# Own slots for the copies of the moved convolution taps, and the layer norm's mean spread one projection later

## The chip, the core and the metric

The kernel runs on one core of one Trainium2 chip. The core has five engines, each with a queue of its own that is worked off in order: PE (TensorE, matrix products), DVE (VectorE), ACT (ScalarE), POOL (GpSimd) and SP (SyncE, which here only issues DMAs). POOL issues the DMAs that add to their destination. They all work on one on-chip memory; 16 DMA engines move data. The metric is the device time of one execution in microseconds (us), lower is better.

## The reference

Two layers. Layer 0 mixes positions by two groups of convolutions, layer 1 by stick-breaking attention; each is followed by a gated ConvFFN. Sequence 1024, width 1024, everything in float32. The change lies in the mixer of layer 0:

```python
def conv_mixer(h, w_in, a_dw_w, a_dw_b, a_ln_g, a_ln_b, b_dw_w, w_out):
    p = h @ w_in
    a_val, a_gate, b_gb, b_gc, b_h = jnp.split(
        p, [D_A, 2 * D_A, 2 * D_A + D_B, 2 * D_A + 2 * D_B], axis=-1)
    a = causal_dwconv(a_val * jax.nn.sigmoid(a_gate), a_dw_w, a_dw_b)   # width 31
    a = jax.nn.silu(layernorm(a, a_ln_g, a_ln_b))
    b = b_gb * causal_dwconv(b_gc * b_h, b_dw_w)                        # width 3
    return jnp.concatenate([a, b], axis=-1) @ w_out
```

D_A and D_B are 512, so the input projection has 2560 columns, 20 blocks of 128.

## The kernel before

Channels lie on the 128 partitions, the 1024 positions along the free axis. A tensor of 128 x 1024 floats is one slot; `Mem` hands out 38 slots by number (t16 to t53; the names in the rows carry slot and allocation, t44_551 is slot 44), oldest freed first. Who writes into a slot waits until the previous owner's last reader is done, a DMA included.

Every float32 product is made of three passes (`mm3`, lines 644 to 646) over a high and a low part of each operand. So each weight slot is split: ACT casts the high part (line 628), DVE subtracts to get the low part (line 629). `W.pump` keeps loads and splits some projections ahead.

`mixer0` runs the 20 projections n = 0 to 19, here p0 to p19; one is 48 matmuls into one of three PSUM tiles (b0, b1, bb0, taken in turn, so that pn needs the tile of p(n-3) read out). p0 to p7 are gate and value of the four channel blocks j of group A: after each value, `conv_taps` queues the 31-wide convolution of the block. 20 of its taps are multiply-adds on DVE (`dtap`, line 838). 10 are moved off it: two initialise two sums, eight (`mtap`, lines 841 to 845) are a scaled copy by ACT into a slot (line 843) and a DMA issued by POOL that adds the slot to one of the two sums in turn (line 844); a merge adds one sum to the other (line 848), and `fin` (line 858) adds them to DVE's part. I call the four convolutions c0 to c3 and the eight added copies of one its adds 1 to 8. An add waits for the add before it on the same sum, so two are in flight.

p8 to p19 are the three projections of each block of group B: gc is copied by ACT (line 1102), h is multiplied in by DVE (line 1104) and convolved (lines 815, 819), gb is multiplied in (line 1109), then the result is split. Before p17, `b_out` puts the first three blocks of B through their part of the output projection.

The layer norm of A goes in four steps after projections: `ln0` after p14 finishes all taps and sums the four blocks (lines 1009 to 1011), `ln1` after p15 spreads the mean over the partitions by a matmul with ones (line 1016, `spread`), subtracts it (line 1032), squares and sums; `ln2` after p16 spreads the variance; `ln3` after p17 spreads the inverse root (line 1016), scales (1052), applies swish (1054, 1055, 1057) and splits the four parts of A. After p19 `back_all` multiplies these four parts and the last part of B by their output weights, eight row tiles one after the other.

The engines' instructions stand in an order that a scheduler wrote at build time; each engine keeps to it. Line numbers below line 843 are one to three higher in the changed kernel.

Of the kernel before, what the change touches and what calls it, by code (L numbers as in the profile page):

```python
# [152 lines left out]
class Up:  # L153
# [12 lines left out]
    def __init__(self, k, l):  # L166
        self.k, self.l = k, l
        self.raw, self.S, self.A, self.a1, self.done1 = {}, {}, {}, {}, {}
        self.rb, self.ys, self.T = [None] * 4, {}, {}
# [40 lines left out]
    def split2(self, f):  # L210
# [8 lines left out]
        m.free(v)  # L219
        self.A[f] = s12, s34, a22  # L220

# [145 lines left out]
    def block(self, f):  # L367

        k, m, nc = self.k, self.k.m, self.k.nc
        if f + 2 < NF and f + 2 not in self.raw:  # L370
            self.load(f + 2)
        if f not in self.A:
            self.split2(f)
# [4 lines left out]
        lo, hi = slice(0, 512), slice(512, 1024)  # L378
        (s12h, s12l), (s34h, s34l), a22 = self.A.pop(f)
        H, L, H3, L3, A2 = [m.ap(s) for s in (s12h, s12l, s34h, s34l, a22)]  # L380
# [238 lines left out]
class Kern:  # L619
# [203 lines left out]
    def conv_taps(self, j, u, acc, sums):  # L823


        nc, m = self.nc, self.m
        w = [self.const(self.col["aw"] + k * NJ + j) for k in range(CW)]
        U, A, B = m.ap(u), m.ap(acc), [m.ap(s) for s in sums]
        shifts = list(range(1, CW))
        moved, dve = shifts[:MOVED_TAPS], shifts[MOVED_TAPS:]  # L830

        nc.scalar.activation(A, U, AF.Identity, scale=w[CW - 1], bias=self.const(self.col["ab"] + j))
        for s, b in zip(moved, B):
            nc.gpsimd.memset(b[:, 0:s], 0.0)
            nc.scalar.activation(b[:, s:], U[:, :S - s], AF.Copy, scale=w[CW - 1 - s])

        def dtap(s):
            nc.vector.scalar_tensor_tensor(out=A[:, s:], in0=U[:, :S - s], scalar=w[CW - 1 - s],
                                           in1=A[:, s:], op0=ALU.mult, op1=ALU.add)

        def mtap(s, b):
            t = m.alloc()
            nc.scalar.activation(m.ap(t)[:, :S - s], U[:, :S - s], AF.Copy, scale=w[CW - 1 - s])
            nc.gpsimd.dma_start(out=b[:, s:], in_=m.ap(t)[:, :S - s], accum_op=ALU.add)
            m.free(t)

        def merge():
            nc.gpsimd.dma_start(out=B[0], in_=B[1], accum_op=ALU.add)
            m.free(sums[1])

        for s in dve:
            self.dq.append(lambda s=s: dtap(s))
        for i, s in enumerate(moved[2:]):
            self.pq.append(lambda s=s, b=B[i % 2]: mtap(s, b))
        self.pq.append(merge)

        def fin():
            nc.vector.tensor_tensor(out=A, in0=A, in1=B[0], op=ALU.add)
            m.free(u)
            m.free(sums[0])  # L860
            self.conv_done += 1

        self.fq.append((len(self.dq) + self.dn, len(self.pq) + self.pn, fin))
# [118 lines left out]
    def mixer0(self):  # L982
        nc, m, a = self.nc, self.m, self.a
# [18 lines left out]
        self.open_psum("ps0b", 1, 2)  # L1002

        accs, bparts, aparts = [], [], []
        W.reserve = 4


        def total(xs):
            nc.gpsimd.tensor_tensor(out=m.ap(s1), in0=xs[0], in1=xs[1], op=ALU.add)
            nc.vector.tensor_tensor(out=m.ap(s2), in0=xs[2], in1=xs[3], op=ALU.add)  # L1010
            nc.vector.tensor_tensor(out=m.ap(s1), in0=m.ap(s1), in1=m.ap(s2), op=ALU.add)
# [8 lines left out]
        def ln0():  # L1020
            nonlocal s1, s2, A
            self.pop_bg(200, 200)
            assert self.conv_done == NJ
            A = [m.ap(s) for s in accs]
            s1, s2 = m.alloc(), m.alloc()
            total(A)
# [34 lines left out]
            m.free(s2)  # L1061

        s1 = s2 = A = None
        ln = [ln0, ln1, ln2, ln3]
        def b_out(wi):
            W.pump(wi[-1])
            ws = [W.views(q) for q in wi]
            acts = [(m.ap(h), m.ap(l)) for h, l in bparts]
            self.back_all(acts, ws, lambda t: self.pop_bg(2, 1))
            for q in wi:  # L1070
                W.done(q)
            while bparts:
                for q in bparts.pop():
                    m.free(q)

        for n in range(20):
            if n == pb:
                b_out([pb + q for q in range(nb)])
            i = n if n < pb else n + nb
            W.pump(i)  # L1080
            if i < 2:
                ps = self.first[i]
            else:
                ps = self.big()
                for c in range(2):
                    self.proj_chunk(ps, W.views(i), c)
            W.done(i)
            if n < 8:
                j = n // 2
                if n % 2 == 0:  # L1090
                    sg = m.alloc()
                    nc.scalar.activation(m.ap(sg), ps, AF.Sigmoid)
                else:
                    nc.vector.tensor_tensor(out=m.ap(sg), in0=ps, in1=m.ap(sg), op=ALU.mult)
                    acc, sums = m.alloc(), [m.alloc() for _ in range(2)]
                    accs.append(acc)
                    self.conv_taps(j, sg, acc, sums)
            else:
                j, q = divmod(n - 8, 3)
                if q == 0:  # L1100
                    gc = m.alloc()
                    nc.scalar.copy(out=m.ap(gc), in_=ps)
                elif q == 1:
                    nc.vector.tensor_tensor(out=m.ap(gc), in0=ps, in1=m.ap(gc), op=ALU.mult)  # L1104
                    cv = m.alloc()
                    self.conv3(m.ap(cv), m.ap(gc), [self.const(self.col["bw"] + k * NJ + j) for k in range(3)], None)
                    m.free(gc)
                else:
                    nc.vector.tensor_tensor(out=m.ap(cv), in0=ps, in1=m.ap(cv), op=ALU.mult)
                    bparts.append(self.split(cv))  # L1110
            self.pop_bg(6, 3)
            if 14 <= n < 18:
                ln[n - 14]()

        gain = self.load_gain(a["ffn_norm_g"][0:1, :].rearrange("o d -> (o d)"))
        W.reserve = 2
# [506 lines left out]
```

## Time and profile before

| | |
|---|---|
| median of 3 runs | 2321.15 us (2319.4 to 2325.52) |
| the profiled execution, device time | 2319.02 us |
| its span in the trace | 2317.2 us |
| mean granted TensorE clock | 0.993 |
| busy share of the span | PE 96%, DVE 75%, ACT 54%, POOL 24% |

The profile's times count from the span's start. The device time holds 1.8 us around the span. A row of a timeline gives start and duration, engine, line, operation, output and inputs, and in brackets how long the engine had been idle and what released it.

### The profile page before, as it was taken

Reading aid. Unit: us, or ns where it says so; the run is one execution under the profiler, and the core shown is the slowest. Engines: PE = TensorE matmul, PEld = TensorE weight load, DVE = VectorE, ACT = ScalarE, POOL = GpSimd, SP = SyncE. Lnnn points to the kernel's source line nnn. Section 1 sums busy time; section 2 is a strip of 40 time slices with the busy share of each in tenths; the row PEclk is TensorE's granted clock in tenths of the full one; section 3 lists DMA queues with packets and bytes.
Section 4 is the critical chain, followed back from the end, with each engine's and each line's share of the span. In section 5 each row is a group of like instructions: output and inputs, shape, how many; then the busy total and the mean of one; then the engine's idle time right before and its main releaser. Section 6 shows DMA issues by size and latency. Waiting matters only on the chain. (4 is left out here: it accounts for less than half of the span.)

```text
span 2317.2 us, 29706 instructions
## 1 busy us (share of the span) xinstructions
PE 2232.6 (96%) x11076; PEld 1908.4 (82%) x11076; DVE 1726.5 (75%) x2023; ACT 1262.6 (54%) x1978; POOL 561.8 (24%) x551
## 2 busy tenths in 40 slices
PE   8998999999999999999999999989999999999999
PEld 8886887888788888889999999978777888888887
DVE  6879457877686887556888888887668777778863
ACT  6433246555555543436677677765566565655341
POOL 2221012111111000035555555562121121110000
PEclk9999999999999999999999999999999999999999
DMA  5984146767676494321111110034476767666812
GB/s 178 190 174 99 35 127 144 191 144 193 148 186 155 146 386 168 103 80 28 37 28 37 37 37 10 28 106 152 130 162 166 192 149 196 145 177 249 332 51 109
DMA packets 247826, 313.00 MB, mean 135 GB/s; under 512 B 12557, under 2 KB 170753, under 8 KB 247681
## 3 DMA queue, kind: packets, MB, share of 16 engines
q1 hardware_dynamic: 214977, 238.32, 31.0%
q0 software_dynamic: 32704, 72.78, 17.7%
q8 instruction: 87, 1.43, 0.2%
q14 instruction: 58, 0.48, 0.1%
HBM read 181.14 MB, written 60.82 MB: 104 GB/s over the span
## 5 line engine op out<-in xcount | busy, mean ns | idle before, releaser
L199 POOL DMA_DIRECT2D t<-t x176 | 155.8, 978 | 701.2 <-ACT t L194 271.3
L628 ACT CAST t<-t 128x1024 fp32r<-128x1024 f32 x178 | 184.9, 1048 | 223.9 <-DMA hs<-t 62.0
L819 DVE SCALAR_TENSOR_TENSOR t<-t,cst,t 128x1023 f32<-128x1023 f32 (+1 forms) x184 | 236.1, 1286 | 81.9 <-ACT t L817 76.7
L629 DVE TENSOR_TENSOR t<-t,t 128x1024 fp32r<-128x1024 f32 x178 | 219.1, 1237 | 101.0 <-ACT t L628 47.2
L1274 DVE TENSOR_TENSOR_SCAN t<-t 128x127 f32<-128x127 f32 (+7 forms) x128 | 204.1, 1600 | 6.9 <-ACT t L1265 6.8
L644 PE MATMUL ps1s<-wH,hH 128*128 128x384 f32 x448 | 165.8, 370 | 0.0
L646 PE MATMUL ps0b<-hH,t 128*128 128x512 f32 x396 | 154.6, 391 | 3.5 <-DVE t L629 3.4
L644 PE MATMUL ps0b<-hH,t 128*128 128x512 f32 x396 | 155.8, 395 | 1.9 <-DVE t L1104 1.4
L645 PE MATMUL ps0b<-hL,t 128*128 128x512 f32 x396 | 154.7, 391 | 0.0
L710 POOL TENSOR_TENSOR stat<-stat,mhalf 128x8 f32<-128x8 f32 (+1 forms) x65 | 80.2, 1234 | 299.9 <-DVE stat L709 299.7
L646 PE MATMUL ps1s<-wH,hL 128*128 128x384 f32 x448 | 151.1, 337 | 0.0
L1279 POOL TENSOR_TENSOR t<-t,t 128x639 f32<-128x639 f32 (+1 forms) x64 | 108.6, 1697 | 175.1 <-DVE t L1274 103.7
L645 PE MATMUL ps1s<-wL,hH 128*128 128x384 f32 x448 | 150.9, 337 | 0.0
L817 ACT ACTIVATE t<-t,cst 128x1024 f32<-128x1024 f32 x88 | 109.1, 1240 | 66.3 <-DVE t L392 47.4
L645 PE MATMUL ps2b<-t,t 128*128 128x512 f32 x342 | 133.9, 392 | 3.9 <-DMA t<-t 3.9
L644 PE MATMUL ps2b<-t,t 128*128 128x512 f32 x342 | 134.0, 392 | 3.3 <-ACT t L394 1.6
L646 PE MATMUL ps2b<-t,t 128*128 128x512 f32 x342 | 132.7, 390 | 0.0
L1265 ACT ACTIVATE t<-ps1s 128x512 f32<-128x512 f32 (+1 forms) x192 | 95.4, 497 | 54.7 <-PE ps1s L1261 28.3
L1297 ACT CAST t<-ps1s 128x512 fp32r<-128x512 f32 (+1 forms) x160 | 87.3, 546 | 60.9 <-PE ps1s L1293 53.5
L1298 DVE TENSOR_TENSOR t<-ps1s,t 128x512 fp32r<-128x512 f32 (+1 forms) x160 | 100.2, 627 | 21.0 <-ACT t L1297 18.8
L517 ACT CAST hH<-t 128x1024 fp32r<-128x1024 f32 x64 | 64.4, 1051 | 86.4 <-PE ps0bs L645 19.6
L517 ACT CAST hL<-t 128x1024 fp32r<-128x1024 f32 x64 | 64.3, 1051 | 86.3 <-PE ps2s L645 25.3
(348 smaller groups left out, 6480.7 us busy)
## 6 DMA issues: line engine op xcount, KB each, us to landing
t<-in_ffn_w_up_dram SPq DMA_DIRECT2D x88, 512.0 KB
t<-t POOLq DMA_DIRECT2D x176, 256.0 KB, 4.4
t<-hs SPq DMA_DIRECT2D x66, 512.0 KB
hs<-t SPq DMA_DIRECT2D x60, 512.0 KB
t<-in_ffn_w_down_dram SPq DMA_DIRECT2D x66, 256.0 KB
xd<-t SPq DMA_DIRECT2D x24, 512.0 KB
wr<-in_attn_w_qkv_dram SPq DMA_DIRECT2D x24, 512.0 KB
t<-in_ffn_w_up_dram SPq DMA_DIRECT2D x44, 256.0 KB
```

The source lines that it names most:

```text
L199: nc.gpsimd.dma_start(out=out, in_=src, accum_op=ALU.add)
L517: nc.scalar.copy(out=r(m.ap(h)), in_=src)
L628: nc.scalar.copy(out=r(m.ap(h)), in_=m.ap(src))
L629: (eng or nc.vector).tensor_tensor(out=r(m.ap(l)), in0=m.ap(src), in1=m.ap(h), op=ALU.subtract)
L644: mm(out=ps, lhsT=sH, rhs=mH, start=start, stop=False, skip_group_check=onto)
L645: mm(out=ps, lhsT=sH, rhs=mL, start=False, stop=False, skip_group_check=onto)
L646: mm(out=ps, lhsT=sL, rhs=mH, start=False, stop=stop, skip_group_check=onto)
L817: nc.scalar.activation(dst, src, AF.Identity, scale=wcols[2], bias=bias)
L819: nc.vector.scalar_tensor_tensor(out=dst[:, s:], in0=src[:, :S - s], scalar=wcols[2 - s], in1=dst[:, s:], op0=ALU.mult, op1=ALU.add)
L1274: self.nc.vector.tensor_tensor_scan(out=rev, data0=rev, data1=rev, initial=1.0, op0=ALU.mult, op1=ALU.bypass)
L1279: self.nc.gpsimd.tensor_tensor(out=B[:, 0:n - 1], in0=B[:, 0:n - 1], in1=K[:, 1:n], op=ALU.mult)
L1298: nc.vector.tensor_tensor(out=r(aL), in0=ps[:, 0:pos], in1=aH, op=ALU.subtract)
```

## The change

The scaled copies of `mtap` no longer take and free a slot each: four slots are taken once, before the projections, and used in turn, and are freed when `ln0` begins. Three of the four steps of the layer norm move by one projection: the mean is spread after p16, the variance after p17, the inverse root after p18.

```diff
         def mtap(s, b):
-            t = m.alloc()
+            t = self.copies[self.ncopy % len(self.copies)]
+            self.ncopy += 1
             nc.scalar.activation(m.ap(t)[:, :S - s], U[:, :S - s], AF.Copy, scale=w[CW - 1 - s])
             nc.gpsimd.dma_start(out=b[:, s:], in_=m.ap(t)[:, :S - s], accum_op=ALU.add)
-            m.free(t)
...
         accs, bparts, aparts = [], [], []
+        self.copies, self.ncopy = [m.alloc() for _ in range(4)], 0
         W.reserve = 4
...
             assert self.conv_done == NJ
+            for s in self.copies:
+                m.free(s)
...
-        ln = [ln0, ln1, ln2, ln3]
+        ln = {14: ln0, 16: ln1, 17: ln2, 18: ln3}
...
-            if 14 <= n < 18:
-                ln[n - 14]()
+            if n in ln:
+                ln[n]()
```

The scheduler writes the whole mixer in another order. Three places:

PE, the spreading of the mean. Before, it stands between p15 (tile b1) and p16 (tile b0):

```order
L645 MATMUL ps0b1_72<-hL_67,t30_1393 128x512
L646 MATMUL ps0b1_72<-hH_66,t37_1394 128x512
L1016 MATMUL ps0bb0_548<-t51_1515,tmp_87 128x512 x2
L644 MATMUL ps0b0_71<-hH_66,t47_1458 128x512
L645 MATMUL ps0b0_71<-hL_67,t47_1458 128x512
```

Now it stands behind p16 (tile bb0) and is followed by the first products of `b_out`:

```order
L645 MATMUL ps0bb0_548<-hL_67,t37_1430 128x512
L646 MATMUL ps0bb0_548<-hH_66,t31_1431 128x512
L1017 MATMUL ps0b0_71<-t35_1487,tmp_87 128x512 x2
L644 MATMUL ps0b1_72<-t36_1494,t52_1208 128x512
L645 MATMUL ps0b1_72<-t50_1495,t52_1208 128x512
```

The 48 matmuls of p16 have moved ahead of it.

ACT, the copies of c3 (inputs t26_936 before, t25_926 now) and the splits of weights around them. Before, the high part of p12 (t51_1175) stands eight rows ahead of these, among c2's copies, and here come the copy of p8's result (L1102), c3's copies out of their order, each into a slot of its own, c2's last copy (t36_1169) and the split for p13 (t50_1250):

```order
L1102 COPY t32_1084<-ps0b0_71 128x1024
L843 ACTIVATE t45_1384<-t26_936,cst_177 128x1015
L843 ACTIVATE t44_1387<-t26_936,cst_177 128x1014
L843 ACTIVATE t38_1316<-t26_936,cst_177 128x1016
L843 ACTIVATE t36_1169<-t53_786,cst_177 128x1014
L628 CAST t50_1250<-t37_1101 128x1024
L843 ACTIVATE t36_1310<-t26_936,cst_177 128x1018
```

Now c3's adds 5 to 8 are copied into slots 44 to 47, each of which its adds 1 to 4 read, and the high parts for p12 (t31_1155), p13 and p14 stand behind all of them:

```order
L1105 COPY t35_1069<-ps0b0_71 128x1024
L844 ACTIVATE t44_551<-t25_926,cst_177 128x1017
L844 ACTIVATE t45_552<-t25_926,cst_177 128x1016
L844 ACTIVATE t46_553<-t25_926,cst_177 128x1015
L844 ACTIVATE t47_554<-t25_926,cst_177 128x1014
L628 CAST t31_1155<-t42_1015 128x1024
L628 CAST t36_1227<-t24_1083 128x1024
L628 CAST t42_1295<-t37_1153 128x1024
```

The split for p12 has moved from the copies of c2 to behind the last copy of c3.

DVE, the low part for p12 and the multiplication that reads p9's tile b1. Before, the low part (t33_1176) comes nine rows ahead of it (L1104):

```order
L629 TENSOR_TENSOR t33_1176<-t38_1030,t51_1175 128x1024
L838 SCALAR_TENSOR_TENSOR t24_711<-t36_639,cst_177,t24_711 128x996
L838 SCALAR_TENSOR_TENSOR t42_1006<-t26_936,cst_177,t42_1006 128x1011
L838 SCALAR_TENSOR_TENSOR t41_859<-t53_786,cst_177,t41_859 128x1003
L838 SCALAR_TENSOR_TENSOR t24_711<-t36_639,cst_177,t24_711 128x995
L838 SCALAR_TENSOR_TENSOR t42_1006<-t26_936,cst_177,t42_1006 128x1010
L838 SCALAR_TENSOR_TENSOR t41_859<-t53_786,cst_177,t41_859 128x1002
L838 SCALAR_TENSOR_TENSOR t24_711<-t36_639,cst_177,t24_711 128x994
L858 TENSOR_TENSOR t24_711<-t24_711,t27_712 128x1024
L838 SCALAR_TENSOR_TENSOR t42_1006<-t26_936,cst_177,t42_1006 128x1009
L1104 TENSOR_TENSOR t32_1084<-ps0b1_72,t32_1084 128x1024
```

Now it (t51_1156) comes three rows ahead of it (L1107):

```order
L858 TENSOR_TENSOR t43_709<-t43_709,t31_710 128x1024
L838 SCALAR_TENSOR_TENSOR t32_994<-t25_926,cst_177,t32_994 128x1010
L838 SCALAR_TENSOR_TENSOR t48_852<-t28_782,cst_177,t48_852 128x1001
L629 TENSOR_TENSOR t51_1156<-t42_1015,t31_1155 128x1024
L838 SCALAR_TENSOR_TENSOR t32_994<-t25_926,cst_177,t32_994 128x1009
L838 SCALAR_TENSOR_TENSOR t48_852<-t28_782,cst_177,t48_852 128x1000
L1107 TENSOR_TENSOR t35_1069<-ps0b1_72,t35_1069 128x1024
```

The multiplication and every tap after it now stand behind a split that waits for ACT's cast of t31_1155.

## Rows read from the trace of the kernel before

**Rows 1.** The page's first part: busy time, share of the span and instructions of an engine.
```profile
PE 2232.6 (96%) x11076; PEld 1908.4 (82%) x11076; DVE 1726.5 (75%) x2023; ACT 1262.6 (54%) x1978; POOL 561.8 (24%) x551
```
**Rows 2.** Stretches of the mixer: start:end, length, busy us (instructions) of PE, PE's weight loads, DVE, ACT and POOL, then granted clock, DMA share, GB/s.
```profile
130.00:140.00 10.00, 10.00 (x46) 8.29 (x45) 10.00 (x9) 7.70 (x8) 3.52 (x4) 1.00 1.02 189
...
180.00:190.00 10.00, 6.93 (x30) 5.37 (x30) 10.00 (x7) 0.00 (x0) 3.29 (x2) 1.00 0.73 144
190.00:200.00 10.00, 8.23 (x35) 6.22 (x34) 10.00 (x9) 3.15 (x3) 0.00 (x0) 1.00 0.18 52
200.00:210.00 10.00, 7.45 (x33) 5.82 (x31) 9.87 (x10) 3.95 (x4) 0.00 (x0) 1.00 0.29 87
210.00:220.00 10.00, 6.42 (x12) 3.78 (x13) 9.39 (x9) 2.42 (x3) 0.00 (x0) 0.66 0.07 20
220.00:230.00 10.00, 10.00 (x45) 8.25 (x44) 10.00 (x8) 5.07 (x5) 2.41 (x1) 1.00 0.41 116
```
**Rows 3.** Timeline of PE: the first matmul of p11, of p12 and of p13, the waits after it, the mean's spreading, p16, the first matmul of `b_out`, and the spreading in `ln3` with the matmul after it.
```profile
145.56 0.39 PE L644 MATMUL ps0b<-hH,t 128*128 128x512 f32 x1
156.44 0.39 PE L644 MATMUL ps0b<-hH,t 128*128 128x512 f32 x1
168.22 0.47 PE L644 MATMUL ps0bb<-hH,t 128*128 128x512 f32 x1 [0.74 <-DVE t L1109]
183.50 0.50 PE L646 MATMUL ps0b<-hH,t 128*128 128x512 f32 x1 [3.07 <-DVE t L629]
195.67 0.47 PE L644 MATMUL ps0b<-hH,t 128*128 128x512 f32 x1 [1.43 <-DVE t L1104]
213.58 3.78 PE L1016 MATMUL ps0bb<-t,tmp 128*128 128x512 f32 x4 [6.13 <-DVE t L1011]
216.37 1.42 PE L644 MATMUL ps0b<-hH,t 128*128 128x512 f32 x1
229.14 0.39 PE L644 MATMUL ps0bb<-t,t 128*128 128x512 f32 x1
274.43 1.88 PE L1016 MATMUL ps0bb<-t,tmp 128*128 128x512 f32 x4
275.74 0.79 PE L644 MATMUL ps0b<-hH,t 128*128 128x512 f32 x1
```
**Rows 4.** Who waited for whom from 45 to 240 us: engine, tile, line, what was waited for: us in total, times, longest.
```profile
DVE t L629 <- DMA t<-t: 14.4, 3, 6.6
...
ACT t L843 <- DMA t<-t: 35.4, 11, 8.0
```
**Rows 5.** Timeline of DVE: ten taps in a row, and the sum of the four blocks, for which the mean's spreading waits.
```profile
100.63 11.99 DVE L838 SCALAR_TENSOR_TENSOR t<-t,cst,t 128x1006 f32<-128x1006 f32 x10
...
212.30 1.23 DVE L1011 TENSOR_TENSOR t<-t,t 128x1024 f32<-128x1024 f32 x1
```
**Rows 6.** Timeline of POOL: c0's adds 1 and 2, its merge; c1's add 1 and 5, its merge; c2's adds 1 and 2, its adds 3 and 4.
```profile
53.83 1.96 POOL L844 DMA_DIRECT2D t<-t  x2 [9.59 <-ACT t L843]
80.00 0.88 POOL L848 DMA_DIRECT2D t<-t  x1 [4.47 <-DMA t<-t]
85.10 0.87 POOL L844 DMA_DIRECT2D t<-t  x1 [4.11 <-ACT t L843]
99.55 0.87 POOL L844 DMA_DIRECT2D t<-t  x1 [3.05 <-DMA t<-t]
114.57 0.87 POOL L848 DMA_DIRECT2D t<-t  x1 [5.14 <-DMA t<-t]
115.12 2.16 POOL L844 DMA_DIRECT2D t<-t  x2
122.47 0.87 POOL L844 DMA_DIRECT2D t<-t  x1 [5.18 <-ACT t L1092]
125.04 0.87 POOL L844 DMA_DIRECT2D t<-t  x1 [1.70 <-DMA t<-t]
```
**Rows 7.** The adds' line: time from issue to landing.
```profile
DMA to landing us min/median/max: 4.5/5.7/11.9
```
**Rows 8.** Groups of instructions from 45 to 213 us: count, busy us and mean ns of one, idle time before them.
```profile
L629 DVE TENSOR_TENSOR t<-t,t 128x1024 fp32r<-128x1024 f32 x14 | 17.0, 1220 | 23.6 <-DMA t<-t 14.4 <-ACT t L628 9.2
L1104 DVE TENSOR_TENSOR t<-ps0b,t 128x1024 f32<-128x1024 f32 x2 | 2.4, 1214 | 0.0
L843 ACT ACTIVATE t<-t,cst 128x1021 f32<-128x1021 f32 (+7 forms) x32 | 34.9, 1138 | 35.4 <-DMA t<-t 35.4
L628 ACT CAST t<-t 128x1024 fp32r<-128x1024 f32 x16 | 16.4, 1044 | 42.7 <-DVE t L858 16.2 <-DMA t<-in_conv_w_in_dram 9.3 <-DVE t L1109 8.0
```
**Rows 9.** Timelines of DVE, ACT and PE after the spreading in `ln3` (274.43): scaling, sigmoid, the split of the first part, the low parts of the last part and of a weight, the first matmul of `back_all`.
```profile
276.35 4.61 DVE L1052 TENSOR_TENSOR t<-t,ps0bb 128x1024 f32<-128x1024 f32 x4 [10.51 <-PE ps0bb L1016]
277.60 2.38 ACT L1054 ACTIVATE t<-t,cst 128x1024 f32<-128x1024 f32 x2 [1.96 <-DVE t L1052]
285.56 1.99 ACT L628 CAST t<-t 128x1024 fp32r<-128x1024 f32 x2
296.16 2.35 DVE L629 TENSOR_TENSOR t<-t,t 128x1024 fp32r<-128x1024 f32 x2
297.95 0.39 PE L644 MATMUL ps0bb<-t,t 128*128 128x512 f32 x1
```

## The prediction, made before the changed kernel ran

> **What bounds the kernel now.** I read the profile's first part first: PE is busy 96% of the span and DVE, the next, 75% [rows 1]. A change gains only where PE idles or runs slowly, and loses where it makes PE wait. So I looked for PE's waits where the change works. From the start of b_out at 229.14 until some time after back_all's start at 297.95 there is none; ahead of it there are four [rows 3]: p13 waits 0.74 for L1109, p14 3.07 for a low weight part of DVE, p15 1.43 for L1104, and the mean's spreading 6.13 for L1011 on DVE.
>
> The last costs twice. After it the granted clock is 0.66 in 210:220 [rows 2], a mixture of 1.2 and 2.4 GHz. The spreading takes 2.79 until p16 starts (213.58 to 216.37) against 1.31 for the one in ln3 (274.43 to 275.74), and p16 takes 12.77 (216.37 to 229.14) against 10.88 for p11 (145.56 to 156.44) [rows 3]: 1.48 + 1.89 = 3.4 us of slow clock. The 3.07 wait was followed by a stretch at 1.00 [rows 2].
>
> What could be had at most: p12 to p16 and one spreading at full rate take 5 x 10.88 + 1.31 = 55.7; from p12's start at 156.44 that ends at 212.15, and b_out starts at 229.14. **The headroom is 17.0 us.** Some 11.4 of it are the four waits, 3.4 the clock, the rest slow first matmuls behind waits.
>
> DVE is the engine that is late: it is busy 9.4 to 10 of every 10 us shown from 180 on [rows 2]. Yet between 45 and 240 its low splits waited 14.4 us, three times, for a DMA, at most 6.6 at once, and ACT's copies at L843 waited 35.4 us for DMAs, 11 times [rows 4]. Those are waits for slots that something else had used.
>
> **Own slots: what they remove.** No instruction is added or removed. Each adding DMA now holds a slot that only other copies want, so the splits no longer wait for an add's landing, and the 14.4 us of DVE should go. With DVE that much earlier, the waits of p13 to p15 and of the mean lose their cause.
>
> **The mean one projection later: what it removes.** Now PE may do p16 before the mean. The sum L1011 (213.5 at its end [rows 5]) then has 10.88 us more, so the 6.13 wait and its 3.4 of clock are gone so long as DVE doesn't get much later. These two parts could give the whole 17.0.
>
> **What they add.** The order shows a new chain. ACT's copies for c3's adds 5 to 8 reuse the slots of its adds 1 to 4, and each must wait until its slot's add has landed. The high part for p12 stands behind all four on ACT; the low part stands on DVE just ahead of two taps and L1107, which reads out p9's tile b1, and p12 needs that tile. All later taps are queued behind it too. Before, that split stood among c2's copies. So I need the landing of c3's add 4.
>
> c0's merge is issued at 80.00, and nothing ahead of it moves. A convolution takes 26.2 from its first add to its merge (53.83 to 80.00) or 29.5 (85.10 to 114.57), and the next may start 0.55 later (114.57 to 115.12) [rows 6]. Two more convolutions put c2's merge at 80.00 + 2 x 26.75 = 133.5 at the earliest and 80.00 + 2 x 30.05 = 140.1 at the latest. c3's add 4 is issued 0.55 + 9.92 (115.12 to 125.04 [rows 6]) later, at 144.0 to 150.6, and lands 4.5 to 5.7 after that (minimum and median; maximum 11.9 [rows 7]): 148.5 to 156.3, or 162.5 at worst. I take 156.3, the late end, because the DMA engines had no share left over in 130:140 (1.02 [rows 2]) when c2's adds ran there, and the order puts c3's adds among weight loads.
>
> Behind the landing: a copy 1.14, the high split 1.04, the low split 1.2 [rows 8], two taps at 1.2 [rows 5], L1107 1.2 [rows 8], together 7.0. L1107 ends at 163.3, while PE wants p12 at 156.44: **a wait of 6.9 us**, with bounds of 0 (landing at 148.5: 155.5) and 13.1 (landing at 162.5). p13 needs L1112 of p10, eleven DVE instructions behind L1107: 11 x 1.18 = 13.0, so 176.3 instead of 167.32. That is 9.0 late. The clock probably falls again as after the 6.13 wait, but the slow p12 (163.3 + 12.8 = 176.1) fits into p13's wait. With all 3.4 of clock it would be 163.3 + 10.88 + 3.4 = 177.6, 10.3 late. **I take 9.5 lost**, and nothing lost after p13: L1011 stands 39 instructions behind L1107, 39 x 1.2 = 47, so the sum is ready at 210, and PE arrives at the spreading at 156.44 + 54.4 + 9.5 = 220.3. The 10 us between are also what covers the cost of moving the mean; if DVE were more than 10 us later still, the old wait would return. b_out starts 17.0 - 9.5 = 7.5 earlier than now.
>
> A rule of the Trainium skill, "DMA: Bandwidth & Descriptors", section "Issuing engines are not separate DMA queues", speaks against a quicker chain of adds: DMAs from whichever engine end up on the same 16 DMA engines and interleave, so four slots more buy no more transfer rate. The row that agrees is the share of 1.02 in 130:140 [rows 2]. By that rule the landing is at the late end, as taken; without it, at 148.5, the wait would be nothing.
>
> **The inverse root one projection later: what it costs.** Before, p18 and p19 covered ln3's work between its spreading and back_all. Now only p19 does, which ends 1.31 + 10.88 = 12.2 after the spreading's start. Counted from that start in the trace of before: L1052 at 1.92, the sigmoid at 3.17, the first part's split from 11.13 [rows 9] until 12.2 [rows 8]. In the new order, DVE then takes L1112 of p19, which needs p19's end: 12.2 + 1.2 = 13.4. Seven low splits follow at 1.17 (two in 2.35 [rows 9]): the seventh, the low part of the fourth output weight, ends at 21.6. Ahead of the matmuls that need it PE has 30 of earlier parts, 30 x 0.227 = 6.8 (10.88 over 48), until 12.2 + 6.8 = 19.0. **Cost 2.6.** Bounds: 0 if DVE finds time for splits earlier; 10.7 if it takes as long as before, 22.9 from the spreading to that weight's low part (274.43 to 297.3, the second of the two splits [rows 9]), with nothing between p19's end and it. I take 2.6 because the order does leave those matmuls there.
>
> **Sum.** -17.0 + 9.5 + 2.6 = -4.9. The profiled execution took 2319.0, so 2314.1; the median of the runs is 2.1 above that execution, so **2316**. What a measurement of this kernel can tell from no change is about 0.3%, 7 us.
>
> **The rivals.**
> *No new wait.* The adds run at the quick pace (26.2, landing 4.5), c3's add 4 lands by 149.5, and L1107 is done before PE wants it. Then -17.0 + 2.6 = -14.4: median 2306.7. For it: nothing but adds uses those slots now, and ACT's 35.4 us of waiting [rows 4] were partly what held the adds up, such as the 4.11 ahead of c1's first [rows 6]. Against: the full DMA engines.
> *The tail costs its upper bound*, and own slots only move the wait: -17.0 + 9.5 + 10.7 = +3.2, median 2324.3. For it: ACT and DVE in ln3 depend on each other from step to step. Against: a DVE that is earlier elsewhere.
> *Slower.* c3's adds 2 and 4, in series on one sum, each land only after the maximum, 11.9, instead of 5.7. Then add 4 lands at 156.3 + 2 x 6.2 = 168.7, L1107 ends at 175.7, p13 starts at 188.7, 21.4 late, and the net is -17.0 + 21.4 + 2.6 = +7.0: median 2328.2. The gain is gone from a landing of 161.7 on. For it: landings of 11.9 do occur [rows 7] where loads share the engines. Against: the median is half that, and two in a row are needed.
> That the change doesn't do what it says would need the mean's sum over 10 us later than worked out above; I count that in with the slower one.
>
> "TensorE: Matmul & The Clock Gate" of the Trainium skill, Part 1, has the clock fall to 1.2 GHz when PE has been idle. The trace agrees after the 6.13 wait (0.66 in the next row [rows 2]), while after the 3.07 wait the row stays at 1.00. By that rule the slow clock follows the new 6.9 wait too, which is the 10.3 bound above instead of 9.5: a total of 2317 rather than 2316.
>
> **How the numbers follow.** Forecast 0.50, no new wait 0.25, tail at its bound 0.15, slower 0.10. The forecast lies 2 us short of 0.3% faster, so about 0.13 of its 0.50 falls beyond: faster 0.25 + 0.13 = 0.38. The slower case lies at +7.0, on the bound: with its worse half and a share of the tail's, slower 0.10. Same: the remaining 0.52. The range goes from the quick case's time, 2306, to between the tail's and the slower case's, 2326. The forecast's own is 2312 to 2321 (bounds of the wait and the clock).
>
> **What would show it.** Right: ACT's L844 waiting for an adding DMA between 140 and 157; DVE's L629 waiting many us for ACT's L628 there; PE waiting about 7 us for L1107 at p12's start and again for L1112 at p13's; no wait at the mean's spreading, which starts near 220; b_out near 221.6; a short wait for L629 in back_all's first products. Wrong: p12 starting at 156.4 (the first rival), a wait of some 10 us at back_all (the second), p12 starting beyond 169 or a wait left at the mean (the third).

## The result, and the profile after

The changed kernel is slower: 2331.49 us in the median (2328.38 to 2336.45), against 2322.29 of the kernel before in the same comparison. The ratio is 1.0043, 95% interval 1.0027 to 1.0058. The forecast was 2316 with a range to 2326, so it was wrong in size and in sign. The profiled execution has a span of 2328.5 us, 11.3 more than the one before. I follow the difference by the start of the same matmul in both traces: +2.2 at p11, +17.7 at p12, +3.0 at b_out, +8.5 in the last row tile of back_all. The rest of the 11.3, 2.8 us, gathers far behind the mixer, where nothing was changed; the medians differ by 9.2.

PE of the changed kernel: its waits, the spreading of the mean (230.86) and of the inverse root (289.13). They answer to [rows 3]. Columns: start, duration, engine, line, operation, tiles; in brackets the wait before it and what ended it.

```profile
147.72 0.50 PE L644 MATMUL ps0b<-hH,t 128*128 128x512 f32 x1 [0.42 <-ACT t L1105]
174.14 0.77 PE L644 MATMUL ps0b<-hH,t 128*128 128x512 f32 x1 [15.23 <-DVE t L1107]
187.34 0.39 PE L644 MATMUL ps0bb<-hH,t 128*128 128x512 f32 x1
230.86 1.88 PE L1017 MATMUL ps0b<-t,tmp 128*128 128x512 f32 x4
289.13 1.88 PE L1017 MATMUL ps0b<-t,tmp 128*128 128x512 f32 x4
304.10 0.50 PE L644 MATMUL ps0b<-t,t 128*128 128x512 f32 x1 [1.18 <-DVE t L1112]
306.40 0.50 PE L646 MATMUL ps0bb<-t,t 128*128 128x512 f32 x1 [1.57 <-DVE t L629]
310.94 0.50 PE L645 MATMUL ps0bb<-t,t 128*128 128x512 f32 x1 [0.84 <-DVE t L629]
```

The four waits of before, 11.4 us in all, are gone, the 6.13 at the mean among them. One of 15.2 at p12's start has come in their place, and it costs the clock too: p12 takes 13.20 (174.14 to 187.34) instead of 10.88, and the granted clock, the third number from the right, says why: 0.59 and 0.56 from 160 to 180 (columns as in [rows 2]):

```profile
140.00:150.00 10.00, 9.58 (x43) 7.61 (x42) 7.28 (x7) 3.20 (x3) 2.90 (x4) 1.00 0.59 110
150.00:160.00 10.00, 8.90 (x40) 7.04 (x38) 0.00 (x0) 2.29 (x2) 1.76 (x2) 1.00 1.09 217
160.00:170.00 10.00, 0.00 (x0) 0.00 (x0) 0.72 (x1) 3.96 (x4) 1.75 (x2) 0.59 1.03 228
170.00:180.00 10.00, 5.86 (x16) 4.71 (x17) 10.00 (x10) 2.39 (x3) 2.65 (x3) 0.56 0.75 138
180.00:190.00 10.00, 10.00 (x46) 8.26 (x45) 10.00 (x9) 3.02 (x3) 0.00 (x0) 1.00 0.27 52
```

DVE does nothing at all from 150 to 160, ACT a quarter of the time: neither is short of time, both wait. ACT's timeline (c3's copies 5 to 8, then the high parts for p12 and p13) and DVE's (the low part for p12, two taps, L1107) show the chain, link by link:

```profile
153.67 1.15 ACT L844 ACTIVATE t<-t,cst 128x1017 f32<-128x1017 f32 x1 [6.00 <-DMA t<-t]
157.61 1.14 ACT L844 ACTIVATE t<-t,cst 128x1016 f32<-128x1016 f32 x1 [2.79 <-DMA t<-t]
163.35 1.14 ACT L844 ACTIVATE t<-t,cst 128x1015 f32<-128x1015 f32 x1 [4.60 <-DMA t<-t]
167.18 1.14 ACT L844 ACTIVATE t<-t,cst 128x1014 f32<-128x1014 f32 x1 [2.68 <-DMA t<-t]
168.22 1.97 ACT L628 CAST t<-t 128x1024 fp32r<-128x1024 f32 x2
...
169.28 1.23 DVE L629 TENSOR_TENSOR t<-t,t 128x1024 fp32r<-128x1024 f32 x1 [22.00 <-ACT t L628]
170.42 2.44 DVE L838 SCALAR_TENSOR_TENSOR t<-t,cst,t 128x1009 f32<-128x1009 f32 x2
172.78 1.22 DVE L1107 TENSOR_TENSOR t<-ps0b,t 128x1024 f32<-128x1024 f32 x1
```

Four copies each wait for an add to land, the last until 167.18; the split for p12 follows at 168.22, DVE has waited 22.0 us for it, L1107 ends at 174.0 and p12 starts at 174.14. This is the chain of the prediction; the landing that it waits for comes 10.9 us later than predicted. Where the time went, the adds on POOL say: the first two of a convolution (x2), the third, the merge (L848).

```profile
55.43 1.95 POOL L845 DMA_DIRECT2D t<-t  x2 [3.45 <-ACT t L844]
60.71 0.86 POOL L845 DMA_DIRECT2D t<-t  x1 [3.33 <-DMA t<-t]
74.89 0.89 POOL L845 DMA_DIRECT2D t<-t  x1 [2.08 <-DMA t<-t]
82.35 0.88 POOL L848 DMA_DIRECT2D t<-t  x1 [6.58 <-DMA t<-t]
82.90 2.13 POOL L845 DMA_DIRECT2D t<-t  x2
92.59 0.89 POOL L845 DMA_DIRECT2D t<-t  x1 [7.56 <-DMA t<-t]
...
113.71 0.87 POOL L848 DMA_DIRECT2D t<-t  x1 [4.60 <-DMA t<-t]
114.26 2.15 POOL L845 DMA_DIRECT2D t<-t  x2
121.73 0.87 POOL L845 DMA_DIRECT2D t<-t  x1 [5.31 <-DMA t<-t]
...
146.21 0.89 POOL L848 DMA_DIRECT2D t<-t  x1 [6.00 <-DMA t<-t]
146.75 2.15 POOL L845 DMA_DIRECT2D t<-t  x2
154.23 0.87 POOL L845 DMA_DIRECT2D t<-t  x1 [5.33 <-DMA t<-t]
158.17 0.89 POOL L845 DMA_DIRECT2D t<-t  x1 [3.07 <-DMA t<-t]
```

c0 takes 26.9 from its first add to its merge, c1 30.8, c2 32.0. Within c0, adds follow each other every 2.84 us (60.71 to 74.89, five steps). Where a merge is in flight ahead of a convolution, its third add comes 7.5 to 9.7 after its first; in c0, with no merge ahead, 5.3.

### The profile page after: what moved, and what is told of

Same layout as the page of the kernel before. It is cut to its first block, busy times and chain, and to the rows that moved or that the text cites. A ratio compares the mean times of both kernels' runs of the same rounds, so it can differ in the third digit from the quotient of the medians.

```text
span 2328.5 us, 29722 instructions
## 1 busy us (share of the span) xinstructions
PE 2234.7 (96%) x11076; PEld 1909.1 (82%) x11076; DVE 1726.6 (74%) x2023; ACT 1263.4 (54%) x1978; POOL 563.8 (24%) x551
## 5 line engine op out<-in xcount | busy, mean ns | idle before, releaser
L644 PE MATMUL ps1s<-wH,hH 128*128 128x384 f32 x448 | 165.7, 370 | 0.0
L644 PE MATMUL ps0b<-hH,t 128*128 128x512 f32 x364 | 143.4, 395 | 16.6 <-DVE t L1107 15.2
L646 PE MATMUL ps0b<-hH,t 128*128 128x512 f32 x364 | 142.4, 392 | 0.4 <-DVE t L629 0.3
L645 PE MATMUL ps0b<-hL,t 128*128 128x512 f32 x364 | 142.5, 392 | 0.0
L1300 ACT CAST t<-ps1s 128x512 fp32r<-128x512 f32 (+1 forms) x160 | 87.3, 545 | 61.8 <-PE ps1s L1296 54.4
```

The costliest lines, as they stand in the source:

```text
L644: mm(out=ps, lhsT=sH, rhs=mH, start=start, stop=False, skip_group_check=onto)
L645: mm(out=ps, lhsT=sH, rhs=mL, start=False, stop=False, skip_group_check=onto)
L646: mm(out=ps, lhsT=sL, rhs=mH, start=False, stop=stop, skip_group_check=onto)
```

## The experiments

My theory after the result: the loss is the new chain through ACT's queue (p12's split behind copies that wait for c3's adds), and in addition the late inverse root at back_all. The rivals: the shift of the layer norm alone makes the loss; DVE's time is what counts; the adds are slow because of what else the DMA engines carry.

**The two halves of the change.** The changed kernel with the old places of the layer norm, and the kernel before with the new places:

```
-        ln = {14: ln0, 16: ln1, 17: ln2, 18: ln3}      (e1, slots alone)
+        ln = {14: ln0, 15: ln1, 16: ln2, 17: ln3}

-        ln = [ln0, ln1, ln2, ln3]                      (e2, shift alone, from before)
+        ln = {14: ln0, 16: ln1, 17: ln2, 18: ln3}
...
```

> Own slots, the layer norm where it was before. ACT's order around c3's copies is the one of the changed kernel. If the loss comes from p12's split standing behind c3's copies 5 to 8 (theory): PE waits 13 to 17 us for L1107 at p12's start, as the 15.2 of the changed kernel; later waits (5.2 at p13 to p15, most of the 6.13 at the mean and its 3.4 of clock) are given back; b_out starts 3 to 6 us later than before, back_all has no new wait: 2322 to 2328, 1.001 to 1.002 of before. If the loss comes from the later steps of the layer norm (rival): faster than before by 5 to 10 us, and no wait over 8 us at p12.

> A slot taken for each copy as before, the layer norm's three steps one projection later. Theory: no long wait at p12; the 6.13 wait and its slow clock at the mean vanish (the mean is ready near 213.5, PE reaches it near 218), so b_out starts 9 to 10 us earlier than before; back_all's first products wait as in the changed kernel, where they cost 5.5: a net gain of 4 us (7 with the 2.6 that was predicted for the tail), 0.997 to 0.998 of before. Rival (the shift makes the loss): slower than before by 5 us or more.

e1: 2331.82 us, ratio 1.0033 (1.0020 to 1.0046); at p12 a wait of 14.68 for L1107. e2: 2322.17 us, 1.0000 (0.9991 to 1.0010). So the own slots make the loss, and the rival falls. But e1 is 3.8 above the top of its range. In its trace b_out starts 4.4 later than before, as expected, and the last row tile of back_all is 4.4 later too; the span is 14.9 longer. The other 10 or so gather behind the mixer; why there, no run shows. The mixer's loss is thus only about half of e1's 8.8 in the medians. Nor did the shift gain what I expected of it. PE in e2:

```profile
220.07 1.88 PE L1016 MATMUL ps0b<-t,tmp 128*128 128x512 f32 x4
229.68 0.50 PE L644 MATMUL ps0b<-t,t 128*128 128x512 f32 x1 [1.34 <-DVE t L1032]
...
295.78 0.51 PE L644 MATMUL ps0b<-t,t 128*128 128x512 f32 x1 [1.19 <-DVE t L1109]
298.08 0.50 PE L646 MATMUL ps0bb<-t,t 128*128 128x512 f32 x1 [1.56 <-DVE t L629]
```

The mean waits no more, and b_out starts 7.8 us earlier than before. Then b_out's matmuls wait for tiles that DVE reads late, because it now subtracts the mean beside them, and 5.0 are left at p18 (leaving out one spreading, which comes before p18 there and behind it here). back_all's waits cost 5.4, and nothing is left: its last row tile comes 0.5 later than before.

**Where the tail's cost sits.** The variance is spread straight after b_out, the inverse root after p17 as before; the mean stays after p16. Once without own slots (e5), once in the changed kernel (e10):

```
-        ln = {14: ln0, 16: ln1, 17: ln2, 18: ln3}      (e10; in e5 from [ln0, ln1, ln2, ln3])
+        ln = {14: ln0, 16: ln1, 17: ln3}
...
                 b_out([pb + q for q in range(nb)])
+                ln2()
```

> No own slots; the mean is spread after p16, but the variance straight after b_out (ahead of p17) and the inverse root after p17 as before. If the tail's cost comes from the inverse root standing after p18: no waits at back_all, and the 5 us that shift_only still had in hand at p18 stay: 2316 to 2319, 0.9975 to 0.9985 of before. If the later mean itself is the cost there: no better than shift_only, 0.999 to 1.001.

> The changed kernel, but the variance is spread straight after b_out and the inverse root after p17 as before; own slots and the later mean stay. If the tail's 5.5 us belong to the inverse root standing after p18, and are independent of the wait at p12: the wait of 15 us at p12 stays, no wait at back_all, 2324 to 2327, 1.0005 to 1.002 of before. If back_all's waits come from DVE's lateness after p12: within 2 us of the changed kernel.

e5: 2317.43 us, 0.9980 (0.9966 to 0.9994): faster than before, with no wait at back_all, and 6 us earlier there than before. e10: 2328.52 us, 1.0023 (1.0011 to 1.0035), a median 1.5 above the expected range; it still waits 15.19 at p12, and no longer at back_all. So the tail's cost belongs to the two late steps, the variance after p17 and the inverse root after p18, and not to the later mean or to DVE's lateness after p12. The two were moved together.

**Only the place of p12's split.**

```
-        W.reserve = 4                                  (e3)
+        W.reserve, W.split_ahead = 4, 3
```

> The changed kernel with weights split three projections ahead instead of two; in the order this puts the high part for p12 on ACT ahead of c3's copies, while p9's convolution (L815) stays behind them. Theory: no wait at p12 for L1107; DVE's 22 us wait for ACT's L628 near 147 is gone; p13, whose tile L1112 reads only after that convolution, then waits 5 to 7 us; b_out starts 7 to 10 us earlier than before, and with 5.5 at back_all the net is a gain of 2 to 5 us, 0.998 to 0.999. Rival (the adds' pace or the late norm is the loss, not where the split stands): within 3 us of the changed kernel, 1.003 to 1.005.

2325.30 us, 1.0012 (1.0002 to 1.0023). The wait at p12 is gone. The next instruction in the same queue takes its place, as expected: p9's convolution starts behind c3's last copy.

```profile
165.03 1.14 ACT L844 ACTIVATE t<-t,cst 128x1014 f32<-128x1014 f32 x1 [1.34 <-DMA t<-t]
166.09 1.13 ACT L815 ACTIVATE t<-t,cst 128x1024 f32<-128x1024 f32 x1
...
176.75 0.79 PE L644 MATMUL ps0bb<-hH,t 128*128 128x512 f32 x1 [6.59 <-DVE t L1112]
```

b_out starts 5 us earlier than before instead of 7 to 10, since this order too loses some 2.7 ahead of p13, and the wait of 6.59 costs the clock as well (0.79 for the first matmul; granted 0.76 in 170 to 180); back_all's waits take 6.3. The loss goes down to a quarter; the expected gain didn't come.

**No copy of c3 behind an add of c3.** Four of c3's moved taps go back to DVE:

```
-        moved, dve = shifts[:MOVED_TAPS], shifts[MOVED_TAPS:]     (e4)
+        nm = 6 if j == NJ - 1 else MOVED_TAPS
+        moved, dve = shifts[:nm], shifts[nm:]
```

> The changed kernel with only four taps of c3 moved off DVE: its copies 5 to 8 and their adds are gone, and DVE has four more multiply-adds (4.8 us). No copy of c3 waits for an add of c3, and the high part for p12 follows c3's fourth copy at once. Theory: no wait at p12 or p13; b_out starts 12 to 15 us earlier than before; with 5.5 at back_all a gain of 6 to 10 us, 0.996 to 0.9975. Rival (DVE's time is what counts): the 4.8 us show up at the mean, and the gain over the changed kernel stays under 5 us.

2335.45 us, 1.0049 (1.0035 to 1.0064): a miss. p12 doesn't wait, but p13 does, 16.46:

```profile
148.37 1.05 ACT L628 CAST t<-t 128x1024 fp32r<-128x1024 f32 x1
171.94 2.94 ACT L628 CAST t<-t 128x1024 fp32r<-128x1024 f32 x3 [22.51 <-DMA t<-t]
...
187.04 0.77 PE L644 MATMUL ps0bb<-hH,t 128*128 128x512 f32 x1 [16.46 <-DVE t L1113]
```

With fewer copies, a split of a later weight (p16's) has moved ahead of p13's on ACT, and it is written into the slot that c3's second sum leaves when its merge has landed. The wait is again one for c3's adds, through another slot.

**Eight own slots.** `self.copies` has 8 slots instead of 4 (e6), so that c3's copies wait for c2's adds.

> The changed kernel with eight own slots: c3's copies wait for the landing of c2's adds, not of c3's own. Theory: c3's last copy is made by 150, p12 and p13 don't wait for L1107 or L1112 over 2 us, b_out starts 10 to 14 us earlier than before, back_all costs 5.5: 2314 to 2319, 0.9965 to 0.9985. Rival: the eight slots are missed by the weights; some PE wait of over 5 us for a split that waits for a slot appears between p8 and p16, and the kernel is not faster than before.

2325.09 us, 1.0008 (0.9997 to 1.0019): not the expected gain. c3's last copy is made at 150.5, and p12 and p13 don't wait. But the copies now hold back what stood behind them earlier: the readout of p8's tile by ACT comes at 152.5, and p11, which needs that tile, waits 4.1 for it; p14 waits 2.8 for its split. b_out starts 1 us earlier than before, not 10 to 14.

**What makes the chain of adds long.** Three runs. In e7 each add moves half of the positions; in e9 SP writes three tiles of 512 KB to memory; in e12 weight loads are issued twice:

```
-            nc.gpsimd.dma_start(out=b[:, s:], in_=m.ap(t)[:, :S - s], accum_op=ALU.add)          (e7)
+            nc.gpsimd.dma_start(out=b[:, s:s + 512], in_=m.ap(t)[:, :512], accum_op=ALU.add)

...
                     self.conv_taps(j, sg, acc, sums)                                              (e9)
+                    if j < 3:
+                        nc.sync.dma_start(out=extra[j], in_=m.ap(sg))

-        self.k.nc.sync.dma_start(out=dst, in_=src)                                                (e12)
+        for _ in range(2 if kind == "k" and 7 <= i <= 14 else 1):
+            self.k.nc.sync.dma_start(out=dst, in_=src)
```

> The changed kernel, but every adding DMA of a scaled copy moves only 512 of the positions: half of those additions are left out. The order on ACT and the slots stay. If the chain is long by the bytes that the DMA engines must move (theory): adds follow each other at about 1.5 instead of 2.7 to 3 us, c3's add 4 lands before 145, the 15 us wait at p12 is gone, b_out starts 12 to 15 us earlier than before, and with 5.5 at back_all the time is 2312 to 2317, 0.995 to 0.998. If it is long by each DMA's own latency: landing stays within 1 us of 6.1 in the median, p12 still waits over 8 us, 1.001 to 1.004.

> The changed kernel with three more DMAs of 512 KB on SP's queue: the inputs of c0, c1 and c2 are also written to memory, where nobody reads them. The order on ACT and the slots stay. If the chain of adds is as long as its bytes and those of everything else take on full DMA engines (185 GB/s between 55 and 167 us in the changed kernel): 3 x 2.8 = 8.4 us more, c3's copy 8 is made near 175 instead of 167, the wait for L1107 at p12 grows from 15.2 to 22 to 25, 2338 to 2341, 1.007 to 1.008 of before. If it is long by the latency of one add after the other: the three fit beside it, the wait grows by less than 3 us, 1.003 to 1.0055.

> The changed kernel with the weight loads of p7 to p14 that stand alone on SP's queue issued twice into the same slot: five more loads of 512 KB between 55 and 167 us, ACT's order unchanged. The three extra stores of e9 did not lengthen the chain of adds. If loads do (theory that is left of the bytes): 1.5 to 2.8 us each, c3's copy 8 is made at 175 to 181 instead of 167, the wait for L1107 at p12 grows to 22 us or more, 1.007 to 1.01 of before. If what shares the DMA engines matters little and the adds' own bytes make the chain: copy 8 before 171, the wait 14 to 18 us, 1.003 to 1.006.

e7: 2317.87 us, 0.9974 (0.9964 to 0.9984). Landing falls from 6.1 to 3.6 in the median, the step within c0 from 2.84 to 1.89, and c3's copy 8 is made at 139.46 instead of 167.18. No wait is left from p12 to the mean, and b_out starts 14.4 us earlier than before: the headroom of 17.0 is there, less the 2.6 that this order loses ahead of the mixer. DVE has the same instructions as in the changed kernel, so it isn't DVE's time that counts: the wait is the length of the chain of adds. The step fell less than expected (1.5), and the median is 0.9 above its range. In this trace back_all's last row tile comes 8.7 earlier than before, the end of the span only 1.0: here too the rest is lost behind the mixer.

e9 and e12 refute my theory of what makes it long. e9: 2335.52 us, 1.0056 (1.0039 to 1.0073); e12: 2336.65 us, 1.0063 (1.0046 to 1.0080). c3's copy 8, in the changed kernel, in e9 and in e12:

```profile
167.18 1.14 ACT L844 ACTIVATE t<-t,cst 128x1014 f32<-128x1014 f32 x1 [2.68 <-DMA t<-t]
...
168.02 1.14 ACT L844 ACTIVATE t<-t,cst 128x1014 f32<-128x1014 f32 x1 [2.68 <-DMA t<-t]
...
168.94 1.14 ACT L845 ACTIVATE t<-t,cst 128x1014 f32<-128x1014 f32 x1 [1.49 <-DMA t<-t]
```

Most of the difference in e9 is the start of the first add (56.16 against 55.43). In the same 111.7 us the DMA engines moved 185 GB/s in the changed kernel, 192 in e9 and 197 in e12, at shares of 0.93, 0.94 and 0.97:

```profile
55.40:167.10 111.70, 103.08 (x454) 84.73 (x452) 75.72 (x64) 50.23 (x47) 28.63 (x34) 0.98 0.93 185
...
55.40:167.10 111.70, 103.86 (x457) 85.32 (x455) 76.55 (x64) 51.01 (x48) 28.65 (x34) 0.98 0.94 192
...
55.40:167.10 111.70, 103.62 (x456) 85.13 (x454) 76.34 (x64) 50.70 (x48) 27.98 (x34) 1.00 0.97 197
```

Two more transfers of 512 KB in that window cost nothing that can be seen (the first of e9's three ran before it), four more about 1.2 us together (168.94 less 167.18, less 0.5 for the later first add; a fifth was issued at 164). Who moved what in the 111.7 us, adds and merges (software_dynamic) and loads (hardware_dynamic), as packets, MB and share of the 16 engines, in the changed kernel and in e12:

```profile
q0 software_dynamic: 4511, 16.36, 79.1%
q1 hardware_dynamic: 7424, 4.19, 13.3%
...
q0 software_dynamic: 4410, 16.01, 78.3%
q1 hardware_dynamic: 11680, 5.88, 18.7%
```

The loads moved 1.69 MB more (less than four whole transfers, since the last regular loads came later), the adds 0.35 MB less. So the share near 1 is mostly that of the adds themselves, their pace goes with their own bytes, and other traffic slows it little. The intervals of both ratios overlap with the changed kernel's.

**Versions meant to be faster than both.** e8 combines e3's split, the layer norm of e5, and the first operation of the width-3 convolution on DVE, so that it doesn't stand behind c3's copies; e11 adds e4's four taps:

```
-            nc.scalar.activation(dst, src, AF.Copy, scale=wcols[2])          (e8, e11)
+            nc.vector.tensor_scalar(out=dst, in0=src, scalar1=wcols[2], scalar2=None, op0=ALU.mult)
```

> Own slots, weights split three projections ahead, the first operation of the width-3 convolution on DVE instead of ACT, variance after b_out and inverse root after p17. Theory (ACT's order behind c3's copies is the cost): neither p12 nor p13 waits over 2 us, b_out starts 10 to 13 us earlier than before, no wait at back_all: 2311 to 2315, 0.9955 to 0.997. Rival (only moved on): p13 or p14 waits 5 us or more for a split that stands behind c3's last copy, 0.999 to 1.001.

> The kernel of e8 with only four taps of c3 moved off DVE, so that nothing of c3 waits for c3's own adds (four more multiply-adds on DVE, 4.8 us; in e8 the sum of the mean was ready 11 us ahead of PE). Theory: e8's 2.84 wait for L1113 at p13 goes, nothing else waits, 1 to 4 us less than e8: 2311 to 2314, 0.9945 to 0.996 of before. Rival: a split that waits for the slot of c3's merged sum takes the place, as in e4 (22.5 us on ACT): slower than e8 by 5 us or more.

e8: 2315.17 us, 0.9960 (0.9944 to 0.9975), 0.8% less than the changed kernel by the two ratios, just above its expected range; p13 still waits 2.84, and b_out starts 11 us earlier than before. e11: 2324.39 us, 1.0003 (0.9990 to 1.0016), a miss, and its rival in another queue:

```profile
165.13 0.35 SPq L117 DMA_DIRECT2D t<-in_conv_w_out_dram  x1
165.70 0.99 SPq L117 DMA_DIRECT2D t<-in_conv_w_in_dram  x2
...
172.39 1.99 ACT L628 CAST t<-t 128x1024 fp32r<-128x1024 f32 x2 [28.75 <-DMA t<-in_conv_w_in_dram]
...
179.18 0.79 PE L644 MATMUL ps0bb<-hH,t 128*128 128x512 f32 x1 [10.64 <-DVE t L1114]
```

On SP a load of an output weight into the slot of c3's second sum has come to stand ahead of the loads for p15 and p14. It is issued at 165.13, after the merge that was issued at 160.48, and the two loads right behind it, at 165.7. ACT's casts wait for them, and on DVE the low part for p15 stands ahead of L1114, for which p13 waits.

## Why the prediction was wrong, point by point

*The headroom, 17.0 us:* right. e7, with the wait away, starts b_out 14.4 us earlier with a loss of 2.6 ahead of the mixer.

*What the two parts remove:* right. The waits of p13 to p15 and of the mean are gone, and in e7 they are gone although PE isn't late. The mean's sum is ready at 221.9 against PE's arrival at 230.9, a margin of 9 where 10 was predicted; that the margin fits is partly luck, for both came more than 10 later than predicted.

*The new wait at p12:* its mechanism and its 7.0 us from landing to L1107 were right (6.8: 167.2 to 174.0). **The step that failed is the landing of c3's add 4, taken as 156.3 and measured as 167.2.** Its terms: c0's merge came at 82.35, not 80.00; c1 and c2 took 63.9 to c2's merge (82.35 to 146.21), not at most 60.1; from there to the issue of add 4 12.0, not 10.5; landing 9.0 (158.17 to 167.18), not 5.7. That is 2.3 + 3.8 + 1.5 + 3.3 = 10.9. Of the 2.3, 1.6 is c0's later start (55.43 against 53.83). I put durations of single convolutions of before [rows 6] behind each other. But c0 there has no merge ahead of it, and c1's first add came 5.1 after the merge because it waited for ACT. With own slots every convolution starts 0.55 behind the merge of the one before, and its first adds are issued while it is in flight. The row to look at was c2's of before, which also starts so: its third add came 7.35 after its first (115.12 to 122.47 [rows 6], there put down to ACT), against 9.69, 7.47 and 7.48 now and 5.28 in c0. For c1 that is the whole of its 3.9 over c0; of c2's 5.0 it is 2.2, and the rest is spread over steps of up to 4.3. That the merge is what slows them is argued from these cases; no run leaves a merge out. "At the latest" came from a convolution that starts in another way, and was no bound. The median landing also hid that the second add of a convolution took 8.8 in the median before and takes 10.1 now.

*"Nothing ahead of it moves":* wrong by 2.2 us at p11. With own slots the scheduler puts the split of one more weight ahead of the last row tile's scaling on DVE, before the mixer (PE then waits 1.19 for L721 at 39.20 instead of 0.20 at 37.61), and p11 starts 0.42 behind a tile that ACT reads out late. e1 shows 1.7 of it at the same place (39.27) and e2 0.3 (37.89), so it comes with the slots.

*p13 behind L1112:* not seen. p12 was so late that p13 found its tile free. The clock's cost (2.3 in p12) then fell on the path in full, where I had let it disappear in p13's wait; the upper bound of 10.3 had it. The prediction's sentence on the Trainium skill, "TensorE: Matmul & The Clock Gate", Part 1, points to that bound, and the 0.59 and 0.56 of 160 to 180, after PE had stood idle, agree with its rule.

*The loss from p12 on* is 230.86 - 156.44 - 54.4 = 20.0 instead of 9.5 (17.7 at p12's start and 2.3 of clock): 3.0 more than the headroom, and b_out starts 3.0 later.

*The tail, 2.6:* 5.5 (8.5 at back_all's last row tile less 3.0). L1112 came at 13.7 after the spreading and not at 12.2, behind two multiplications of the swish that had waited 1.20 for ACT; the first of the splits behind it took 2.38 and the seven others 1.21, where I had 1.17 for each; and PE was not busy for 30 matmuls but waited after four, 1.18 for L1112 itself, since one of back_all's row tiles needs the PSUM tile that L1112 reads. The upper bound of 10.7 held, but I had read it too low: the second of the two splits [rows 9] starts at 297.3 and ends at 298.5, which makes 11.9.

*The rivals:* of the three, the slower one came about, with its place (p12), its wait for L1107 and its landing (168.7 put, 167.2 measured), though not by two landings of 11.9 but by the whole chain's pace. I had given it 0.10. That its 168.7 lies near the measured landing is luck. Against it I had set that two slow landings in a row are rare; its condition should have been the pace of three convolutions.

*The rule of the Trainium skill on the queues* ("DMA: Bandwidth & Descriptors", "Issuing engines are not separate DMA queues") I had read as a full set of engines that gives the late end of my bound. The landing was later than that end. e12 shows that transfers which SP adds to the same engines hardly slow POOL's adds, so a share near 1 was no ground for either end. The rule itself, that the DMAs of all issuers share 16 engines, isn't contradicted by that.

What stays open: why one add needs 2.84 us for its 512 KB when more loads fit in beside it, why the first ones behind a merge are so much slower, and what single executions lose behind the mixer. For the adds, fewer transfers in flight from POOL's queue would be a test; it wasn't tried.

## What to carry to other kernels

A buffer of its own takes a waiting transfer out of one engine's way and puts it into the way of whoever fills the buffer: here ACT. Look at what stands behind that instruction on its in-order queue, and place the urgent split ahead of it, as e3 and e8 did; and expect the next one behind it to be the new wait (e4, e6, e11). When a wait is for the end of a chain of transfers, take its pace from the stretch that starts as the new order will start, and give the chain's whole length, not one landing, to the unfavourable case.

## What the runs showed of the hardware that was not expected

The share of the DMA engines says little about room. At a share of 0.93, of which 0.79 was that of the adds and merges themselves, four more transfers of 512 KB in 111.7 us raised it to 0.97 and the rate from 185 to 197 GB/s, and lengthened a chain of 28 adds and 3 merges by about 1.2 us (e12). Halving the adds' own bytes (e7) shortened their step from 2.84 to 1.89, which, as an estimate from these two, is about 0.9 us a step that doesn't go with the bytes and 1.9 that does.
